# A two-layer trunk on one core: P·V read in 256 columns, kept weights and a new bank order in the output projection, two squares summed on TensorE, separate buffers for outgoing sums

## The chip, the core and the metric

The kernel runs on one core of a Trainium2 chip. The metric is the device time of one execution in microseconds (us). Beside the timed runs there is one profiled execution, whose trace gives every time that is read from a row below. The engines are called as in the profile: PE is TensorE (PEld its weight loads), DVE VectorE, ACT ScalarE, POOL GpSimd, SP SyncE. L12 is line 12 of the kernel.

## The reference

Sixteen learned tokens are put ahead of 1024 frames of width 1024; two layers follow. Each layer normalises, projects, runs two groups of heads side by side (a gated linear attention and FoX, a softmax attention with eight heads of 64 and a cumulative forget-gate bias), joins them in one output projection with a residual, and adds a gated feed-forward part with a causal convolution of width 3.

```python
for i in range(DEPTH):
    xn = rms_norm(h, attn_norm[i])
    gq, gk, gv, gr, glr, fq, fk, fv, ff = jnp.split(xn @ w_in[i], cuts, axis=-1)
    ...
    h = h + jnp.concatenate([o_gla, o_fox], axis=-1) @ w_out[i]
    h = h + conv_ffn(rms_norm(h, ffn_norm[i]), w_up[i], conv_w[i], conv_b[i], w_down[i])
return rms_norm(h, final_norm)[:, N_META:]
```

In conv_ffn a product with w_up gives u and g, each is convolved, and silu(g) * u is multiplied by w_down. In FoX the logits are q·k plus c_t − c_s, where c is the cumulative sum of the log forget gates, and the output is softmax(logits) · V.

## The kernel before

**Numbers.** Every fp32 operand is held as two parts, hi = cast(x) and lo = x − hi. A product is three matmuls into one bank of PSUM (mm3): hi·hi on L218, lo·hi on L219, hi·lo on L220. So a weight is loaded by SP into a buffer raw, cast to hi on ACT and subtracted to lo on DVE (weights: L185 and L187), one tile of 128 output columns ahead of its use (stream). In attention it is POOL that subtracts.

**Stages of a layer.** Projections and the linear attention; FoX attention; output projection with the second norm's statistics; up-projection; down-projection. In layer 0 attention lies at 176 to 539 us of the trace, the output projection at 539 to 601, up until 1048, down until 1258.6; in layer 1 attention at 1452 to 1815.5, the projection until 1879, up until 2328.6, down until 2537.

**FoX.** Queries and keys are cut into nine tiles, the first of 112 frames (FIRST) and the others of 116 (FT), and queries go in pairs of tiles, the first one alone. For each head and pair, fox_scores makes scores and probabilities P; fox_transposes turns P through PE, four key tiles at a time, into one tile of PSUM (tr, L690) and splits it into hi and lo in the buffer PT (L332 on ACT, L333 on DVE); fox_av multiplies (L708). PT has the layout key tile, hi or lo, query. A key tile that both query tiles see is read with 232 columns, one that only the second sees with 116. The steps of scores, transposes and P·V are put a few steps apart by fox_schedule, other work (the remaining projections, named mm) fills between them, and within that the framework's scheduler sets the order on each engine.

**Output projection** (the first half of ffn_up). The 1040 frames are two halves h of 520 (516 in layer 1, and 512 in its down-projection), each written in two chunks of half that. Eight tiles m of 128 output columns run per half, in the order (4, 0, 5, 1, 6, 2, 7, 3) in the first half and (0, 4, 1, 5, 2, 6, 3, 7) in the second. Tiles 4 to 7 need eight pieces of weights, in two loads, two casts and two subtractions, in each half anew; of tiles 0 to 3 all but the last piece was multiplied during attention. wout(i, h) takes bank i % 4, adds the residual (L1110), writes h out by POOL (L1111), squares it on ACT (L1116) and adds the squares on DVE (L1117). scale(h) sums over partitions by a matmul with ones (ssq, L1086, in bank 3), and DVE turns that into the norm's factor (L1089 and the rsqrt, L275 to L277). In the second half scale(0) runs after i = 1, and from i = 3 the first operands of up are normalised (first_operand, L1094, L1052, L1053). second_half calls scale(1) within up, then further operands follow (make_t2 and others).

**Down-projection** (down_blocks). Blocks of seven products, in the manner of Strassen's, run in the order of a table; copies on ACT and additions on DVE (L1375, L1376) gather them into two sums u and g per block, and a DMA on POOL adds those to h in memory (L1392, L1394). u and g come from the common slots, from which a generator (prepare) also takes its buffers: it loads gated activations (st, L1261) and splits them into ah and al (L332, L333) for the products to come. pump(n, keep) lets it go n steps if enough slots are free beside keep.

Of the kernel before, what the change touches and what calls it, by code (L numbers as in the profile page):

```python
# [10 lines left out]
F32 = mybir.dt.float32  # L11
# [40 lines left out]
NSPLIT = 4  # L52
# [82 lines left out]
class Kern:  # L135
# [33 lines left out]

    def weights(self, src, slots=None):  # L170
        nc = self.nc
        nk = src.shape[1]
        parts = []
        if slots:
            HI, LO = slots
        for k0 in range(0, nk, 4):
            n = min(4, nk - k0)
            raw = self.wp.tile([128, 4, 128], F32, tag="raw", name="raw", bufs=4)
            nc.sync.dma_start(raw[:, :n, :], src[:, k0:k0 + n, :])
            if slots:  # L180
# [4 lines left out]
            nc.scalar.copy(hi[:, :n, :], raw[:, :n, :])  # L185
            eng = nc.gpsimd if self.att else nc.vector
            eng.tensor_tensor(out=lo[:, :n, :], in0=raw[:, :n, :], in1=hi[:, :n, :].bitcast(F32), op=ALU.subtract)  # L187
            for k in range(n):
                parts.append((hi[:, k, :], lo[:, k, :]))
        return parts  # L190
# [485 lines left out]
    def fox_transposes(self, i, ci, P, PT, qoff, pp):  # L676
# [10 lines left out]
        for j in range(nt):  # L687
            t = 4 * ci + j
            o, w = self.start_of(t) - self.start_of(4 * ci), FT if i else FIRST
            nc.tensor.transpose(tr[:w, j, :rows], P[:rows, o:o + w], id_)  # L690
        self.split(PT[ci][:w, :nt, 0, qs], PT[ci][:w, :nt, 1, qs], tr[:w, :nt, :rows])

    def fox_av(self, e, tiles, q, PT, avs, pp, part):
# [5 lines left out]
        width = FT * (len(tiles) - 1) + self.rows_of(last)  # L699
        for t in range(4 * part, min(4 * part + 4, last + 1)):  # L700
            a = 0 if t <= tiles[0] else FT
            for i in range(2):
                if t == NT - 1:
                    w, x = q["Vm"][:, e, :, :], PT[2][:, i, :]
                else:
                    r = self.rows_of(t)
                    w, x = q["V"][e][:r, t, :, :], PT[part][:r, t - 4 * part, i, a:width]
                nc.tensor.matmul(av[:, a:width], w.rearrange("p a b -> p (a b)"), x,  # L708
                                 start=(t == 0 and i == 0), stop=(t == last and i == 1))
        if last < 4 * part + 4:  # L710
# [117 lines left out]
    def fox_schedule(self, lyr, at, n, p, e, ti, i, tiles, Ps, st, q, ap, pp, mix3):  # L828
        PT = st[e]

        def T_(ci, P):
            def f():
                if ti == len(tiles) - 1 and ci == 0:
                    for key in range(2):
                        PT[key] = ap.tile([FT, 4, 2, 2 * FT], F32R, tag=f"PT{key}", name=f"PT{key}", bufs=1)
# [196 lines left out]
    def ffn_up(self, lyr, mix, hT, pp, fw, halves, o0, during_last):  # L1032
# [49 lines left out]
        def scale(h):  # L1082

            ps, r = bank2("ssq", 3), acc[:, sl[h]]
            for c in range(2):
                nc.tensor.matmul(ps[:, c, :n], self.ones[:], acc[:, halves[h] + c * n:halves[h] + c * n + n],  # L1086
                                 start=True, stop=True)
            vv, y0, a = half(tmp[0], 0), half(tmp[0], 1), half(tmp[1], 0)
# [9 lines left out]
        def wout(i, h):  # L1098
# [3 lines left out]
            def f(w):  # L1102
                if h == 1 and i == KD - 1:
                    ensure(0)
                ps = bank2("wo", i % 4)
                for k in range(len(w)):
# [7 lines left out]
                else:  # L1114
                    t = half(sq, i % 2)
                    nc.scalar.activation(t, x, AF.Square)  # L1116
                    nc.vector.tensor_tensor(out=acc[:, sl[h]], in0=acc[:, sl[h]], in1=t, op=ALU.add)  # L1117
                if h == 0:
# [10 lines left out]
                for k in turn.get(i, ()):  # L1129
                    first_operand(k)  # L1130
            return (self.wm[lyr, M_WO + m][:, k0:KD, :], f)
        self.stream([wout(i, h) for h in range(2) for i in range(KD)])
        for x in mix:
# [219 lines left out]
    def down_blocks(self, lyr, g0, ng, X, pp, fw, halves, after):  # L1353
# [14 lines left out]
        def ensure(i):  # L1368
            while len(ops) < min(i + 1, len(seq)):
                j, p = seq[len(ops)]  # L1370
                ops.append(self.block_operand(wd(2 * j), wd(2 * j + 1), nk, j, p, fw, raws, len(ops) % 2))

        def evacuate(j, p):
            q = st[j]
            add = lambda out, ps: nc.vector.tensor_tensor(out=two(out), in0=ps[:, :, :n], in1=two(out), op=ALU.add)  # L1375
            copy = lambda out: nc.scalar.copy(two(out), q["a"][:, :, :n])  # L1376
            if p == 1:
                q["u"] = s.get(F32, "du")
                copy(q["u"][:, t0])
# [4 lines left out]
            elif p == 7:  # L1384
                q["g"] = s.get(F32, "dg")
                copy(q["g"][:, t1])
                add(q["g"][:, t1], q["x"])
            elif p == 4:
                copy(q["g"][:, t0])
                nc.gpsimd.dma_start(self.hm[2 * j + 1][:, o0:T], q["g"][:, o0:T], accum_op=ALU.add)  # L1390
                s.put(q["g"])
            elif p == 3:  # L1392
                add(q["u"][:, t1], q["x"])
                nc.gpsimd.dma_start(self.hm[2 * j][:, o0:T], q["u"][:, o0:T], accum_op=ALU.add)  # L1394
                s.put(q["u"])
                del st[j]
        def run():
            for i, (j, p) in enumerate(seq):
# [291 lines left out]
```

## Time and profile before

| | |
|---|---|
| runs | 2592.44, 2593.43, 2593.51 us; median 2593.43 |
| profiled execution | 2591.4 us, its span in the trace 2589.6 us |
| PE busy | 2495.7 us of the span (96%) |
| DVE busy | 1786.6 us (69%) |
| ACT busy | 1288.4 us (50%) |
| POOL busy | 432.6 us (17%) |

A row of the timeline has the start of an instruction in us from the span's start, its recorded length, its engine, line and operation with the names of output and input, and in brackets, where the engine was idle before, for how long and what ended that. A PE row is longer than the distance from one matmul to the next, since matmuls overlap: what a stream costs is read from start to start. A row of the grouped lines has the line, the operation, its shapes and count, then the busy time in us and the mean in ns, then the idle time ahead of it with who ended it.

### The profile page before, as it was taken

What the parts mean: (1) busy time and instruction counts of PE and PEld (TensorE: products, weight loads), DVE (VectorE), ACT (ScalarE), POOL (GpSimd) and SP (SyncE); (2) the same over time, 40 slices, a digit from 0 to 9 for tenths busy, and PEclk for the clock granted to TensorE, in tenths of its full rate; (3) what the DMA queues carried; (4) which work ended last, traced back from release to release, by engine and by line L of the source; (5) the groups of instructions that cost most, each with busy time, mean ns of one, the idle gap of its engine ahead of it and who ended that gap; (6) DMA issues with size and microseconds to landing.
All of it is one profiled execution on the core that took longest, in us unless ns stands there. A gap on an engine that the chain in (4) does not pass through costs nothing.

```text
span 2589.6 us, 48743 instructions
## 1 busy us (share of the span) xinstructions
PE 2495.7 (96%) x19278; PEld 2424.9 (94%) x19278; DVE 1786.6 (69%) x3494; ACT 1288.4 (50%) x2745; POOL 432.6 (17%) x598
## 2 busy tenths in 40 slices
PE   8999999898999999999999999999999999999997
PEld 7988999898999999999999899998899999999997
DVE  7656776759877777853665666776697777777535
ACT  7336666635544445641443565665464444455312
POOL 4033334310000000100301233332100000001002
PEclk9999999999999999999999999999999999999998
DMA  3132134342322223863312222143423222257721
GB/s 125 65 89 60 51 93 127 109 145 89 110 75 87 79 79 129 200 165 107 110 50 67 72 78 76 57 146 114 148 70 114 78 74 86 76 162 179 196 61 67
DMA packets 119670, 263.03 MB, mean 102 GB/s; under 512 B 15008, under 2 KB 32672, under 8 KB 119440
## 3 DMA queue, kind: packets, MB, share of 16 engines
q1 hardware_dynamic: 95136, 184.89, 22.8%
q0 software_dynamic: 22432, 72.71, 10.1%
q8 instruction: 151, 2.47, 0.4%
q10 hardware_dynamic: 1872, 2.31, 0.3%
q14 instruction: 79, 0.65, 0.1%
HBM read 179.26 MB, written 67.81 MB: 95 GB/s over the span
## 4 chain that ended last, share of the span: by engine, by line
PE 62%; issue 16%; DVE 13%; ACT 4%; DMA 3%; POOL 1%; SPq 0%; DVEq 0%; POOLq 0%; ACTq 0%
PE mm L218 7%; PE mm L220 6%; PE mm L219 6%; PE up L218 5%; PE up L219 5%; PE up L220 5%; PE down L218 5%; PE down L219 5%; PE down L220 5%; PE av L708 2%; DVE S L657 2%; PE tr L690 2%; ACT P L669 1%; PE wo L218 1%; PE wo L219 1%
## 5 line engine op out<-in xcount | busy, mean ns | idle before, releaser
L218 PE MATMUL up<-x,hi 128*128 128x260 f32 (+1 forms) x2464 | 697.3, 283 | 2.3 <-ACT x L1052 1.6
L220 PE MATMUL up<-x,hi 128*128 128x260 f32 (+1 forms) x2464 | 695.8, 282 | 2.2 <-DVE x L1053 2.2
L219 PE MATMUL up<-x,lo 128*128 128x260 f32 (+1 forms) x2464 | 696.1, 283 | 0.8 <-DVE lo L1029 0.8
L220 PEld LDWEIGHTS up<-x,hi 128*128 128x128 f32 x2464 | 465.5, 189 | 3.1 <-DVE x L1053 3.1
L218 PEld LDWEIGHTS up<-x,hi 128*128 128x128 f32 x2464 | 464.4, 188 | 3.4 <-ACT x L1052 2.2
L219 PEld LDWEIGHTS up<-x,lo 128*128 128x128 f32 x2464 | 464.8, 189 | 1.0 <-DVE lo L1029 1.0
L1029 DVE TENSOR_TENSOR lo<-raw,hi 128x512 fp32r<-128x512 f32 x364 | 249.0, 689 | 171.3 <-ACT hi L1028 171.3
L218 PE MATMUL mm<-xh,hi 128*128 128x348 f32 (+4 forms) x1056 | 364.6, 345 | 0.0
L220 PE MATMUL mm<-xl,hi 128*128 128x348 f32 (+4 forms) x1056 | 340.1, 322 | 0.0
L219 PE MATMUL mm<-xh,lo 128*128 128x348 f32 (+4 forms) x1056 | 339.2, 321 | 0.0
L1028 ACT CAST hi<-raw 128x512 fp32r<-128x512 f32 x364 | 224.5, 620 | 145.0 <-PE up L220 87.4
L185 ACT CAST hi<-raw 128x512 fp32r<-128x512 f32 (+2 forms) x192 | 112.4, 587 | 201.4 <-PE down L220 114.2
L218 PEld LDWEIGHTS mm<-xh,hi 128*128 128x128 f32 x1056 | 200.2, 190 | 5.9 <-issue 5.3
L219 PEld LDWEIGHTS mm<-xh,lo 128*128 128x128 f32 x1056 | 200.1, 190 | 0.4 <-issue 0.3
L220 PEld LDWEIGHTS mm<-xl,hi 128*128 128x128 f32 x1056 | 198.9, 188 | 0.3 <-issue 0.3
L219 PE MATMUL down<-ah,lo 128*128 128x260 f32 (+1 forms) x704 | 198.6, 282 | 0.3 <-DVE lo L187 0.3
L220 PE MATMUL down<-al,hi 128*128 128x260 f32 (+1 forms) x704 | 198.3, 282 | 0.0
L218 PE MATMUL down<-ah,hi 128*128 128x260 f32 (+1 forms) x704 | 198.3, 282 | 0.0
L669 ACT ACTIVATE P<-S,m 116x460 f32<-116x460 f32 (+2 forms) x224 | 124.8, 561 | 100.1 <-DVE m L657 97.9
L333 DVE TENSOR_TENSOR PT<-tr,PT 116x464 fp32r<-116x464 f32 (+3 forms) x240 | 123.0, 516 | 63.2 <-ACT PT L332 62.3
L1222 POOL DMA_DIRECT2D actd<-cv x44 | 23.6, 535 | 763.5 <-DVE cv L1221 742.5
L1011 DVE TENSOR_TENSOR raw<-raw,raw 128x512 f32<-128x512 f32 x198 | 129.9, 689 | 22.4 <-DMA raw<-in_wd_dram 18.4
(276 smaller groups left out, 5901.0 us busy)
## 6 DMA issues: line engine op xcount, KB each, us to landing
raw<-in_wm_dram SPq DMA_DIRECT2D x338, 256.0 KB, 2.8
raw<-in_wd_dram SPq DMA_DIRECT2D x64, 256.0 KB, 3.5
actd<-cv POOLq DMA_DIRECT2D x22, 520.0 KB, 3.0
actd<-cv POOLq DMA_DIRECT2D x22, 512.0 KB, 3.0
cb<-cd SPq DMA_DIRECT2D x16, 520.0 KB, 3.8
st<-actd SPq DMA_DIRECT2D x14, 520.0 KB, 4.8
st<-actd SPq DMA_DIRECT2D x14, 512.0 KB, 5.3
kA<-kA SPq DMA_DIRECT2D x24, 260.0 KB, 4.3
```

Source lines behind the costliest of these rows:

```text
L185: nc.scalar.copy(hi[:, :n, :], raw[:, :n, :])
L218: nc.tensor.matmul(ps, wh, xh[:, c0:c0 + n], start=first, stop=False, skip_group_check=more)
L219: nc.tensor.matmul(ps, wl, xh[:, c0:c0 + n], start=False, stop=False, skip_group_check=more)
L220: nc.tensor.matmul(ps, wh, xl[:, c0:c0 + n], start=False, stop=last, skip_group_check=more)
L333: nc.vector.tensor_tensor(out=lo, in0=src, in1=hi.bitcast(F32), op=ALU.subtract)
L657: nc.vector.tensor_tensor_reduce(out=S[:rows, :n], in0=S[:rows, :n], in1=cb[:rows, c0:k1], scale=1.0, scalar=(BIG if ci == 0 else m[:rows, ...
L669: nc.scalar.activation(P[:rows, :n], S[:rows, :n], AF.Exp, scale=-1.0, bias=m[:rows, nch - 1:nch], accum_out=(den if nch == 1 else d3[:row ...
L690: nc.tensor.transpose(tr[:w, j, :rows], P[:rows, o:o + w], id_)
L708: nc.tensor.matmul(av[:, a:width], w.rearrange("p a b -> p (a b)"), x, start=(t == 0 and i == 0), stop=(t == last and i == 1))
L1011: nc.vector.tensor_tensor(out=q[out][:, :nk, :], in0=q[a][:, :nk, :], in1=q[b][:, :nk, :], op=op)
L1028: nc.scalar.copy(hi[:, :nk, :], src[:, :nk, :])
L1029: nc.vector.tensor_tensor(out=lo[:, :nk, :], in0=src[:, :nk, :], in1=hi[:, :nk, :].bitcast(F32), op=ALU.subtract)
```

## The change

Four edits go together.

1. **P·V.** PT's layout becomes hi or lo, key tile, query, and the four key tiles lie in reverse order. Where both query tiles see a key tile and another tile's data lie behind it, the matmul reads 256 columns: its own 232 and 24 of the neighbour. The 24 extra columns of av aren't copied out. In the first part the order of key tiles is 1, 0, 2, 3, so that the matmul that starts the sum is one of 256 columns. 448 matmuls become longer; 192 keep 232 columns, since their tile lies last.
2. **Output projection.** Banks in the second half go (0, 1, 2, 0, 1, 3, 2, 1) instead of i % 4. The split weights of m = 5 and m = 6 are kept from the first half in buffers of the feed-forward pool (tags raw2, hi2, lo2) and used again in the second.
3. **Squares.** In the second half the squares of the last two tiles aren't added to the others on DVE; scale(1) sums the three parts in PSUM with three matmuls per chunk in place of one.
4. **Down.** u and g come from a ring of four buffers (do) that goes back to the slots only at the end of run, and both calls of pump lose their keep.

```diff
@@ weights
-    def weights(self, src, slots=None):
+    def weights(self, src, slots=None, keep=None):
...
+            elif keep:
+                hi, lo = (keep[0].tile([128, 4, 128], F32R, tag=t, name="keep", bufs=b) for t, b in keep[1])
@@ fox_transposes
-            nc.tensor.transpose(tr[:w, j, :rows], P[:rows, o:o + w], id_)
-        self.split(PT[ci][:w, :nt, 0, qs], PT[ci][:w, :nt, 1, qs], tr[:w, :nt, :rows])
+            nc.tensor.transpose(tr[:w, 3 - j, :rows], P[:rows, o:o + w], id_)
+        at = slice(4 - nt, 4)
+        self.split(PT[ci][:w, 0, at, qs], PT[ci][:w, 1, at, qs], tr[:w, at, :rows])
@@ fox_av
+        if part == 0 and last:
+            ts[:2] = 1, 0
...
+                    if a == 0 and p < 3:
+                        b = 256
+                        x = PT[part][:r, i].rearrange("p a b -> p (a b)")[:, 2 * FT * p:2 * FT * p + b]
+                nc.tensor.matmul(av[:, a:b], w.rearrange("p a b -> p (a b)"), x,
@@ scale
+            parts = [r] + [half(sq, i) for i in range(2) if h]
             for c in range(2):
-                nc.tensor.matmul(ps[:, c, :n], self.ones[:], acc[:, halves[h] + c * n:halves[h] + c * n + n],
-                                 start=True, stop=True)
+                for i, x in enumerate(parts):
+                    nc.tensor.matmul(ps[:, c, :n], self.ones[:], x[:, c * n:c * n + n],
+                                     start=i == 0, stop=i == len(parts) - 1)
@@ wout
-                ps = bank2("wo", i % 4)
+                ps = bank2("wo", (0, 1, 2, 0, 1, 3, 2, 1)[i] if h else i % 4)
...
+                    if not (h and i >= KD - 2):
+                        nc.vector.tensor_tensor(out=acc[:, sl[h]], in0=acc[:, sl[h]], in1=t, op=ALU.add)
...
+        keep = {5: (fw, [("raw2", 7)] * 2), 6: (fw, [("hi2", 3), ("lo2", 3)])}
@@ down_blocks
+        def outgoing():
+            if not ring:
+                ring.extend(s.get(F32, "do") for _ in range(4))
+            ring.append(ring.pop(0))
+            return ring[-1]
...
-                q["u"] = s.get(F32, "du")
+                q["u"] = outgoing()
...
-                    self.pump(1, 3)
+                    self.pump(1)
                 elif j and p == 5:
-                    self.pump(1, 4)
+                    self.pump(1)
+            s.put(*ring)
```

The lines of the kernel after are 3 to 38 higher than before. Three places show how the order moves. First DVE, near the end of the projection's second half: lo is the split of weights (L187 before, L190 after), h<-wo the residual's addition, h<-h,vec,r and x the operands of up, r<-r,sq the sum of squares, L1029 and L1040 the weights of up. Before:

```order
L1110 TENSOR_TENSOR h_5939<-wo,h_5939 128x520
L1053 TENSOR_TENSOR x_7525<-h_7065,x_7523 128x520
L1123 SCALAR_TENSOR_TENSOR dd<-h_5939,vec,gt 128x520
L1117 TENSOR_TENSOR r<-r,sq 128x520
L1053 TENSOR_TENSOR x_7520<-h_5933,x_7518 128x520
L187 TENSOR_TENSOR lo<-raw,hi 128x512 x2
L1110 TENSOR_TENSOR h_5936<-wo,h_5936 128x520
L1094 SCALAR_TENSOR_TENSOR h_5934<-h_5934,vec,r 128x520
L1029 TENSOR_TENSOR lo<-raw,hi 128x512
L1117 TENSOR_TENSOR r<-r,sq 128x520
```

And in the kernel after:

```order
L1123 TENSOR_TENSOR h_5939<-wo,h_5939 128x520
L1064 TENSOR_TENSOR x_7525<-h_5939,x_7523 128x520
L1138 SCALAR_TENSOR_TENSOR dd<-h_5939,vec,gt 128x520
L1132 TENSOR_TENSOR r<-r,sq 128x520
L1107 SCALAR_TENSOR_TENSOR h_7065<-h_7065,vec,r 128x520
L1107 SCALAR_TENSOR_TENSOR h_5933<-h_5933,vec,r 128x520
L190 TENSOR_TENSOR lo<-raw,hi 128x512
L1064 TENSOR_TENSOR x_7525<-h_7065,x_7523 128x520
L1064 TENSOR_TENSOR x_7520<-h_5933,x_7518 128x520
L1123 TENSOR_TENSOR h_5936<-wo,h_5936 128x520
L1107 SCALAR_TENSOR_TENSOR h_5934<-h_5934,vec,r 128x520
L1040 TENSOR_TENSOR lo<-raw,hi 128x512 x2
```

One lo of the last weights stands ahead of two operands where two stood behind them, and the second sum of squares is gone from this piece. The second place is ACT in the down-projection of layer 0, about the copy that frees a bank (du before, do after); ah is the cast of the activations. Before:

```order
L1028 CAST hi<-raw 128x512
L185 CAST hi<-raw 128x512
L332 CAST ah<-st 128x1040 x3
L1376 COPY du<-down 128x520
L332 CAST ah<-st 128x1040 x2
```

After:

```order
L1039 CAST hi<-raw 128x512
L335 CAST ah<-st 128x1040
L188 CAST hi<-raw 128x512
L335 CAST ah<-st 128x1040
L1415 COPY do<-down 128x520
L335 CAST ah<-st 128x1040 x2
```

Two casts of activations stand ahead of the copy in place of three, and a cast of weights lies between them. The third place is PE in attention, one pass of P·V (av) with the scores S of another step and the transposes tr. Before:

```order
L708 MATMUL av<-PT_2540,V_1609 128x232 x6
L654 MATMUL S<-kA_1605,qA_1603 116x460
L708 MATMUL av<-PT_2540,V_1609 128x232
L655 MATMUL S<-kL_1607,qA_1603 116x460
L708 MATMUL av<-PT_2540,V_1609 128x232
```

After:

```order
L719 MATMUL av<-PT_2540,V_1609 128x256 x2
L719 MATMUL av<-PT_2540,V_1609 128x232 x2
L719 MATMUL av<-PT_2540,V_1609 128x256 x2
L657 MATMUL S<-kA_1605,qA_1603 116x460
L719 MATMUL av<-PT_2540,V_1609 128x256
L658 MATMUL S<-kL_1607,qA_1603 116x460
L719 MATMUL av<-PT_2540,V_1609 128x256
```

Six of eight matmuls are longer; their place among the others is the same here.

More of the change, by code (lines that the diff above doesn't have):

```diff
@@ L699, in fox_av @@
         width = FT * (len(tiles) - 1) + self.rows_of(last)
-        for t in range(4 * part, min(4 * part + 4, last + 1)):
-            a = 0 if t <= tiles[0] else FT
+        ts = list(range(4 * part, min(4 * part + 4, last + 1)))
+        if part == 0 and last:
+            ts[:2] = 1, 0
+        for t in ts:
+            a, b = 0 if t <= tiles[0] else FT, width
             for i in range(2):
@@ L1130, in f, with wout_weights @@
                     first_operand(k)
-            return (self.wm[lyr, M_WO + m][:, k0:KD, :], f)
-        self.stream([wout(i, h) for h in range(2) for i in range(KD)])
+            return f
+        keep = {5: (fw, [("raw2", 7)] * 2), 6: (fw, [("hi2", 3), ("lo2", 3)])}
+        kept = {}
+        def wout_weights(h, i):
+            m = orders[h][i]
+            if m in kept:
+                return kept.pop(m)
+            w = self.weights(self.wm[lyr, M_WO + m][:, KD - 1 if m < NSPLIT else 0:KD, :], keep=keep.get(m))
+            if m in keep:
+                kept[m] = w
+            return w
+        todo = [(h, i) for h in range(2) for i in range(KD)]
+        ahead = wout_weights(*todo[0])
+        for this, nxt in zip(todo, todo[1:] + [None]):
+            w, ahead = ahead, nxt and wout_weights(*nxt)
+            wout(this[1], this[0])(w)
         for x in mix:
@@ L1384, in evacuate @@
             elif p == 7:
-                q["g"] = s.get(F32, "dg")
+                q["g"] = outgoing()
                 copy(q["g"][:, t1])
```

13 lines of the change are left out of this document (5 added, 8 removed).

## Prediction

> **What bounds the kernel now.** The sum is made against the profiled execution: 2591.4 us, of which the span in the trace is 2589.6; the median of the runs is 2593.43, 2.0 more, and is added at the end. First comes the page's table of busy time.
>
> ```profile
> PE 2495.7 (96%) x19278; PEld 2424.9 (94%) x19278; DVE 1786.6 (69%) x3494; ACT 1288.4 (50%) x2745; POOL 432.6 (17%) x598
> ```
>
> TensorE (PE) is at work nearly all the time, so every matmul that is added costs its length, and what can be won is the 4% in which PE stands still. The view of windows tells where that is. Its columns are the window, its length, the busy time of PE, PEld, DVE, ACT and POOL, the granted clock, the DMA share and GB/s. The rows are, in layer 0: attention; output projection; start of the up-projection; its rest; down-projection.
>
> ```profile
> 176.00:539.00 363.00, 340.93 (x2377) 324.53 (x2376) 246.64 (x762) 219.57 (x660) 126.11 (x177) 1.00 0.29 90
> 539.00:601.00 62.00, 56.45 (x438) 55.59 (x439) 44.97 (x75) 29.44 (x54) 9.05 (x16) 0.94 0.48 144
> 601.00:660.00 59.00, 56.08 (x455) 54.76 (x454) 58.28 (x88) 36.26 (x58) 2.88 (x4) 1.00 0.24 68
> 660.00:1048.00 388.00, 388.00 (x3248) 388.00 (x3248) 295.71 (x377) 194.06 (x278) 11.55 (x21) 1.00 0.30 99
> 1048.00:1258.60 210.60, 208.07 (x1732) 207.44 (x1731) 114.27 (x152) 75.39 (x117) 14.43 (x17) 1.00 0.55 144
> ```
>
> Attention lacks 22 us of PE, the projection 5.6 with a clock of 0.94, the start of up 2.9 while DVE is busy for 58.28 of 59 us, the rest of up nothing, down 2.5. So in the 120 us after attention DVE sets the pace, and everywhere else PE or the chain of softmax does. The timeline of PE shows the waits of the projection's second half (start, length, engine, line, operation, then in brackets the idle time and who ended it).
>
> ```profile
> 572.91 0.28 PE L220 MATMUL wo<-ml,hi 128*128 128x260 f32 x1
> 575.05 0.36 PE L218 MATMUL wo<-mh,hi 128*128 128x260 f32 x1 [1.86 <-DVE nt L1089]
> ...
> 576.33 0.42 PE L219 MATMUL wo<-mh,lo 128*128 128x260 f32 x1
> ...
> 579.59 0.35 PE L219 MATMUL wo<-mh,lo 128*128 128x260 f32 x1
> ...
> 590.32 0.28 PE L218 MATMUL wo<-mh,hi 128*128 128x260 f32 x1
> 593.82 0.59 PE L219 MATMUL wo<-mh,lo 128*128 128x260 f32 x1 [3.21 <-DVE lo L187]
> 594.20 0.42 PE L220 MATMUL wo<-ml,hi 128*128 128x260 f32 x1
> ...
> 596.80 0.28 PE L220 MATMUL wo<-ml,hi 128*128 128x260 f32 x1
> ...
> 604.46 1.11 PE L1086 MATMUL ssq<-r,ones 128*128 128x260 f32 x4 [0.59 <-DVE r L1117]
> ```
>
> Matmuls otherwise start every 0.12 us. After each of the two long waits they start every 0.22: the 15 starts up to 579.59 take 3.26 us where 1.80 would do, the 12 up to 596.80 take 2.60 instead of 1.44. A wait thus costs its own length and about 1.2 to 1.5 us more.
>
> **The output projection, step by step.** The new bank order takes the bank that DVE's L1089 reads out of the way of the fourth product: the wait of 2.0 us (575.05 − 572.91 − 0.12) and the slow 1.5 behind it go. The kept weights of m = 5 and 6 take away, in the second half of each layer, four loads, four ACT casts and four DVE subtractions (L187). Two of the eight sums of squares (L1117) leave DVE too. The timeline of DVE and the grouped lines of the 121 us give the prices.
>
> ```profile
> 580.26 0.69 DVE L187 TENSOR_TENSOR lo<-raw,hi 128x512 fp32r<-128x512 f32 x1 [1.32 <-ACT hi L185]
> ...
> 584.77 0.70 DVE L1117 TENSOR_TENSOR r<-r,sq 128x520 f32<-128x520 f32 x1
> 585.38 0.70 DVE L1053 TENSOR_TENSOR x<-h,x 128x520 fp32r<-128x520 f32 x1
> 585.99 0.69 DVE L187 TENSOR_TENSOR lo<-raw,hi 128x512 fp32r<-128x512 f32 x1
> 586.59 0.70 DVE L1110 TENSOR_TENSOR h<-wo,h 128x520 f32<-128x520 f32 x1
> ```
> ```profile
> L218 PE MATMUL up<-x,hi 128*128 128x260 f32 x150 | 42.8, 286 | 1.2 <-ACT x L1052 1.2
> L220 PE MATMUL up<-x,hi 128*128 128x260 f32 x150 | 42.5, 283 | 1.1 <-DVE x L1053 1.1
> L219 PE MATMUL wo<-mh,lo 128*128 128x260 f32 x144 | 42.4, 294 | 3.7 <-DVE lo L187 3.7
> ```
>
> DVE starts such an operation every 0.61 us though each is recorded with 0.70. Two accounts follow for one layer. On DVE: 4 × 0.60 for the subtractions, 2 × 0.61 for the sums, and the idle 1.32 at 580.26, which waits for the cast of a weight that is now kept: 4.9 us less from the second half's start to the last operand of up. On PE: 2.0 + 1.5 (first wait), 3.7 + 1.2 + 0.3 (the waits for lo, the slow stretch and the slow restart at 593.82), 0.6 before ssq, 2.3 in the start of up: 11.6 us that could go at most. Against it stand the squares that PE now adds itself: the four ssq matmuls hold PE from 571.43 to 572.12 and some.
>
> ```profile
> 571.43 1.04 PE L1086 MATMUL ssq<-r,ones 128*128 128x260 f32 x4
> 572.12 0.47 PE L218 MATMUL wo<-mh,hi 128*128 128x260 f32 x1
> 572.43 0.28 PE L219 MATMUL wo<-mh,lo 128*128 128x260 f32 x1
> ```
>
> Two fp32 matmuls are four records; by start to start of the last rows they take 0.69 to 0.87 us. Two squares more are eight records, +1.4 to +1.75 us of PE in each layer; I take 1.75. PE's account comes to −9.9 then, DVE's to −4.9. Up's first products wait for DVE, not the other way, and the last such wait is what shifts all the rest of the layer: the smaller of the two counts, **−4.9 a layer, −9.8 in all**. So PE's waits are not all gone: the second lo of m = 7's weights still stands behind a row of evacuations and operands on DVE. Ends: −8 a layer if up's operand sums, which the new order puts between the evacuations, fit in DVE's idle time; −1 if they push x back and only the two sums remain as gain. The loads and casts that go with the kept weights are counted at nothing more than this: both long waits end on DVE, and ACT is busy for 29.44 of the first 62 us.
>
> **P·V at 256 columns.** In each pass of a head, 28 of its 40 matmuls of 232 columns become 256; over 16 of these, 448 of the 640 in these two rows. All 640 and the price:
>
> ```profile
> L708 PE MATMUL av<-PT,V 116*128 116x232 f32 x512 | 88.8, 275 | 0.8 <-DVE PT L333 0.8
> L708 PE MATMUL av<-PT,V 112*128 112x232 f32 x128 | 29.8, 303 | 3.0 <-DVE PT L333 2.1 <-ACT PT L332 0.7
> ```
> ```profile
> 292.84 1.05 PE L708 MATMUL av<-PT,V 116*128 116x232 f32 x8
> 293.74 0.46 PE L690 MATMUL tr<-ident,P 116*116 116x116 f32 x3
> ```
> ```profile
> 2479.89 0.28 PE L218 MATMUL down<-ah,hi 128*128 128x256 f32 x1
> ...
> 2480.95 0.28 PE L218 MATMUL down<-ah,hi 128*128 128x256 f32 x1
> ```
>
> Eight of 232 columns take 0.90 us, 0.112 each; nine starts of 256 columns take 1.06, 0.118 each. So 448 × 0.006 = **+2.7 us**, on the path, as PE is the bound between its waits. Nothing in the trace says that 232 columns run at a worse rate than 256, so no gain stands against it. Ends: 0, where the added columns fall into time in which PE would have waited (22 us of attention), and +5. The Trainium skill (TensorE: Matmul & The Clock Gate, Back-to-back issue gap) speaks against this edit more strongly: it gives N/2.4 + 2.5 ns for a warm, isolated matmul of N columns, 10 ns more for 256 than for 232. By it the 448 would cost 4.5 us; the rows above show 6 ns, and the sum keeps those.
>
> In attention the order on DVE, ACT and POOL shifts as well, since a scheduler places it. No row prices that; I take 0, with ±4 us as the ends, about a tenth of what PE lacks in attention, if layer 1's is like layer 0's 22 us.
>
> **Down.** The sums that leave get buffers of their own, and the preparation of the gated activations runs one step at a time between products. The timelines of PE (layers 0 and 1) and of ACT:
>
> ```profile
> 1155.38 0.28 PE L220 MATMUL down<-x,hi 128*128 128x260 f32 x1
> 1156.83 0.39 PE L218 MATMUL down<-x,hi 128*128 128x260 f32 x1 [1.17 <-ACT du L1376]
> ...
> 2436.96 0.38 PE L218 MATMUL down<-x,hi 128*128 128x256 f32 x1 [1.42 <-ACT du L1376]
> ```
> ```profile
> 1155.22 1.06 ACT L332 CAST ah<-st 128x1040 fp32r<-128x1040 f32 x1 [0.37 <-DMA st<-actd]
> 1156.19 0.58 ACT L1376 COPY du<-down 128x520 f32<-128x520 f32 x1
> ```
>
> The copy that frees PE's bank stands behind a cast of 1.06 us that itself waited for a load. In the new order that cast comes after the copy. PE's start moves by 1156.83 − 1155.38 − 0.12 = 1.3 us in layer 0, and by 1.4 and the same 0.2 of restart in layer 1: **−2.9 us**. Ends: −4 (smaller waits for the same buffers go too) and 0 (the copy meets another cast).
>
> **Sum.** 2591.4 − 9.8 + 2.7 − 2.9 = 2581.4, and with 2.0 to the median of runs 2583.4: about **2583 us**, −0.4%. Differences under 0.2% (5.2 us) are about what a measurement of this kernel can't tell from none: below 2588.2 is faster, above 2598.6 slower.
>
> **The rivals.**
> - *The start of up keeps its end.* The kept weights free DVE in the second half, but in the order up's operands (L1029, L1011) have moved between the evacuations, and DVE at 58.28 of 59 us has no room for what is early: x arrives as late as now. The 4.9 shrinks to 1, the price of 2 sums: 2591.4 − 2 + 2.7 − 2.9 + 2.0 = 2591, no change. For it: the DVE window. Against: the same operations are only earlier, and four of them do not exist any more. Chance 0.15.
> - *Down meets its loads.* Between one block and the next ACT has waited much longer than 0.37 for what the preparation needs:
>
> ```profile
> 1132.46 1.06 ACT L332 CAST ah<-st 128x1040 fp32r<-128x1040 f32 x1 [4.85 <-DMA hm<-dg]
> ```
>
>   ACT works in order; if the copy of u now stood behind such a cast in each layer, 2 × 4.85 would come in place of −2.9: 2591.4 − 9.8 + 2.7 + 9.7 + 2.0 = 2596, no change. Against it: with buffers of their own the outgoing sums are no longer what that cast waits for. Chance 0.05.
> - *Attention gets slower.* Its chain of scores, softmax, transposes and P·V has PE waiting in these groups of the view of waits (layer 0: engine, line, for whom, total us, times, longest):
>
> ```profile
> PE tr L690 <- DVE PT L333: 10.4, 10, 2.2
> PE S L654 <- ACT P L669: 5.7, 5, 1.5
> ```
>
>   If the shifted order and the longer P·V doubled the first group, ten more waits of 1.04 us in each layer would cost 20.8: 2581.4 + 20.8 + 2.0 = 2604, slower. It decides from 15.2 us on, 7 to 8 such waits a layer. For it: DVE and ACT rows change places all through attention, and PE has no work of its own to bridge a wait there. Against: the splits, transposes and P·V keep their number and their groups. Chance 0.08.
>
> **How the numbers follow.** Forecast 0.72 (its own range 2574 to 2590: −8 a layer, −4 in down and P·V at 0 give 2573; −3 a layer and +3 in attention give 2590), of which a little, 0.02, lies within 0.2% of now; rivals 0.15, 0.05 and 0.08. The range 2574 to 2595 takes in the first rival and leaves out the last and half of the second, with some 0.05 below. Faster: 0.70 and 0.04 of the first rival's lower end, 0.74. Slower: 0.08. Same: 0.18.
>
> **What would show it.** In the projection PE no longer waits for DVE's nt after its third product, and no matmuls at 0.22 us follow; the last wait of up's start comes about 5 us sooner after attention; ssq has eight more records a layer and no wait before them. In attention a stretch between 0 and 3 us longer in each layer, with 448 rows of 256 columns. In down, PE's waits for the copy of u at 1.2 and 1.4 us gone, those of 0.7 for the copy of g as now. Wrong it is if the 121 us after attention shrink by under 2 us a layer, or if attention moves by more than 4 us a layer either way.

## The result and the profile after

The changed kernel takes 2579.8 us (median of four runs, 2576.27 to 2583.94) against 2593.47 before: the ratio is 0.9939, interval 0.9925 to 0.9953, so 12 to 19 us faster. The profiled execution has a span of 2577.6 us in place of 2589.6. The forecast was 2583 us, from 2574 to 2595. The total is near it, but two of its parts are far off.

The page's busy times first. PE is busy for 5.6 us longer, with the wider matmuls of P·V and the squares that it adds, in a span that is 12.0 us shorter.

```profile
PE 2501.3 (97%) x19294; PEld 2430.9 (94%) x19294; DVE 1776.4 (69%) x3482; ACT 1279.6 (50%) x2737; POOL 432.4 (17%) x598
```

Next the windows of the kernel after, cut at the first matmul of each stage: attention, projection, up's start and down of layer 0, then attention, projection and down of layer 1 (columns as above).

```profile
179.71:531.99 352.28, 338.41 (x2334) 321.79 (x2331) 244.11 (x758) 218.51 (x655) 124.03 (x176) 1.00 0.29 88
531.99:586.04 54.05, 53.08 (x437) 52.65 (x437) 36.72 (x62) 22.18 (x42) 10.02 (x17) 1.00 0.53 165
586.04:645.00 58.96, 56.51 (x449) 54.74 (x448) 58.83 (x91) 38.03 (x62) 2.34 (x3) 1.00 0.25 73
1034.84:1248.91 214.07, 209.15 (x1731) 208.66 (x1729) 114.17 (x152) 74.72 (x117) 14.34 (x17) 0.99 0.55 144
1450.06:1801.87 351.81, 336.86 (x2333) 320.20 (x2330) 243.58 (x758) 218.20 (x655) 124.22 (x176) 1.00 0.29 88
1801.87:1858.28 56.41, 54.32 (x436) 53.92 (x437) 37.41 (x63) 23.51 (x45) 10.00 (x17) 0.98 0.51 164
2308.98:2526.34 217.36, 208.04 (x1730) 207.22 (x1729) 113.43 (x150) 73.94 (x115) 14.42 (x17) 0.98 0.52 133
```

Cut the same way, the kernel before has these rows for its two attentions and the down of layer 1 (its projections, so cut, are 61.97 and 63.70 us, its first down 210.50):

```profile
180.98:538.88 357.90, 335.84 (x2333) 319.86 (x2331) 243.21 (x755) 217.04 (x651) 125.06 (x177) 1.00 0.29 90
1458.12:1815.46 357.34, 335.76 (x2334) 319.75 (x2331) 242.85 (x755) 217.00 (x651) 125.22 (x177) 1.00 0.30 90
2328.57:2537.26 208.69, 205.33 (x1730) 204.29 (x1729) 112.22 (x149) 73.84 (x114) 14.41 (x17) 1.00 0.53 138
```

Read the second column. Attention is 5.6 and 5.5 us shorter although PE is busy for longer in it: what PE lacks falls from 22 to 14 us in layer 0 and to 15 in layer 1. The projection is 7.9 and 7.3 shorter, with its clock at 1.00 and 0.98; the up stage behind it is 1.6 and 1.3 longer (447.2 to 448.8 and 449.4 to 450.7), which together makes −6.3 and −6.0 a layer. Down is 3.6 and 8.7 us *longer*. The three sums are −11.1, −12.3 and +12.3.

In the second half of the projection only one long wait of PE is left in each layer, 0.97 us in layer 0 and 2.09 in layer 1. The squares that PE adds follow up's products without a wait (timeline of PE, both waits, then the squares in layer 0):

```profile
581.92 0.28 PE L221 MATMUL wo<-mh,hi 128*128 128x260 f32 x1
583.17 0.39 PE L222 MATMUL wo<-mh,lo 128*128 128x260 f32 x1 [0.97 <-DVE lo L190]
...
1854.30 0.39 PE L222 MATMUL wo<-mh,lo 128*128 128x258 f32 x1 [2.09 <-DVE lo L190]
```
```profile
589.12 0.60 PE L1099 MATMUL ssq<-r,ones 128*128 128x260 f32 x2
...
591.56 0.47 PE L221 MATMUL up<-x,hi 128*128 128x260 f32 x1
```

From the first of twelve ssq records to up's next matmul it is 2.44 us; four took 0.69 to 0.87, so the new eight cost 1.6 to 1.75, as reckoned. The last wait for an operand in the start of up (the two rows below, of the kernel before and of the kernel after) ends 103.7 us after the projection's first matmul before (538.88) and 97.4 us after it now (531.99), 6.4 sooner; in layer 1 it is 5.5 sooner. DVE stays busy for 58.83 of the 58.96 us there.

```profile
642.61 0.39 PE L220 MATMUL up<-x,hi 128*128 128x260 f32 x1 [0.39 <-DVE x L1053]
```
```profile
629.36 0.39 PE L223 MATMUL up<-x,hi 128*128 128x260 f32 x1 [0.38 <-DVE x L1064]
```

In down the waits have changed places and grown (PE in layer 0 and twice in layer 1, then ACT about the first of them):

```profile
1149.61 0.59 PE L221 MATMUL down<-x,hi 128*128 128x260 f32 x1 [4.24 <-ACT do L1415]
...
2356.23 0.39 PE L221 MATMUL down<-x,hi 128*128 128x256 f32 x1 [3.07 <-ACT do L1415]
...
2428.26 0.39 PE L221 MATMUL down<-x,hi 128*128 128x256 f32 x1 [4.15 <-ACT do L1415]
```
```profile
1139.67 0.59 ACT L1415 COPY do<-down 128x520 f32<-128x520 f32 x1 [0.42 <-PE down L223]
1145.58 2.02 ACT L335 CAST ah<-st 128x1040 fp32r<-128x1040 f32 x2 [5.31 <-DMA st<-actd]
...
1148.02 1.05 ACT L335 CAST ah<-st 128x1040 fp32r<-128x1040 f32 x1
1148.98 0.58 ACT L1415 COPY do<-down 128x520 f32<-128x520 f32 x1
```

The copy at 1139.67 is early now, as forecast. But the two casts that were moved behind it stand ahead of the *next* copy, and they wait 5.31 us for their loads. That is the second rival, whose price per layer was a wait of 4.85. At the next copy's product PE had waited 0.68 us before; now it waits 4.24 and 4.15. The wait of 3.07 in layer 1 stands at a product that had none.

The waits are not the whole price. Behind each of these three the granted clock is halved for 3.4 us, from the end of the wait on in layer 0 and 0.9 to 1.3 us later in layer 1; matmuls start 0.21 us apart there in place of 0.12, as behind the long waits of the old projection. That costs some 1.5 us each time. Two windows of layer 1 show the clock:

```profile
2357.50:2360.90 3.40, 3.40 (x19) 3.40 (x18) 2.64 (x5) 1.50 (x3) 0.00 (x0) 0.50 0.04 16
2429.20:2432.60 3.40, 3.40 (x18) 3.40 (x17) 1.23 (x1) 1.05 (x1) 0.00 (x0) 0.50 1.00 401
```

In layer 1 PE's waits of over 0.25 us sum to 9.3 us after and 3.4 before. The difference and twice 1.5 for the clock make 9 us, against the 8.7 by which the stage grew.

### The profile page after: what moved, and what is told of

It reads as the page before. It is cut to its first block, busy times and chain, and to the rows that moved or that the text cites. A ratio compares the mean times of both kernels' runs of the same rounds, so it can differ in the third digit from the quotient of the medians.

```text
span 2577.6 us, 48764 instructions
## 1 busy us (share of the span) xinstructions
PE 2501.3 (97%) x19294; PEld 2430.9 (94%) x19294; DVE 1776.4 (69%) x3482; ACT 1279.6 (50%) x2737; POOL 432.4 (17%) x598
## 4 chain that ended last, share of the span: by engine, by line
PE 63%; issue 16%; DVE 13%; ACT 4%; DMA 3%; POOL 1%; SPq 0%; DVEq 0%; POOLq 0%; ACTq 0%
PE mm L221 7%; PE mm L222 7%; PE mm L223 7%; PE up L221 5%; PE up L222 5%; PE up L223 5%; PE down L221 5%; PE down L222 5%; PE down L223 5%; PE av L719 2%; PE tr L693 2%; DVE S L660 2%; ACT P L672 1%; DVE x L1064 1%; PE S L657 1%
## 5 line engine op out<-in xcount | busy, mean ns | idle before, releaser
L1040 DVE TENSOR_TENSOR lo<-raw,hi 128x512 fp32r<-128x512 f32 x364 | 248.1, 686 | 178.3 <-ACT hi L1039 175.5
L188 ACT CAST hi<-raw 128x512 fp32r<-128x512 f32 (+2 forms) x176 | 102.2, 582 | 190.2 <-PE down L223 108.1
L672 ACT ACTIVATE P<-S,m 116x460 f32<-116x460 f32 (+2 forms) x224 | 124.9, 561 | 79.4 <-DVE m L660 75.7
L336 DVE TENSOR_TENSOR PT<-tr,PT 116x464 fp32r<-116x464 f32 (+3 forms) x240 | 123.4, 515 | 48.4 <-ACT PT L335 46.5
L221 PE MATMUL down<-x,hi 128*128 128x260 f32 (+1 forms) x448 | 128.8, 288 | 12.8 <-ACT do L1415 12.8
```

The lines of the kernel that those rows point to most:

```text
L221: nc.tensor.matmul(ps, wh, xh[:, c0:c0 + n], start=first, stop=False, skip_group_check=more)
L336: nc.vector.tensor_tensor(out=lo, in0=src, in1=hi.bitcast(F32), op=ALU.subtract)
L672: nc.scalar.activation(P[:rows, :n], S[:rows, :n], AF.Exp, scale=-1.0, bias=m[:rows, nch - 1:nch], accum_out=(den if nch == 1 else d3[:row ...
L1040: nc.vector.tensor_tensor(out=lo[:, :nk, :], in0=src[:, :nk, :], in1=hi[:, :nk, :].bitcast(F32), op=ALU.subtract)
```

## The experiments

Stage lengths below are read like those above, from the first matmul of one stage to that of the next. "Projection and up" runs from the first wo matmul to the first of down: 509.2 and 513.1 us before. The expectation of the run bank has 609.2 and 613.1 for it, 100 us too much; the differences that it argues with are not touched by that. In the three other kernels that leave this part alone the stage takes 507.5 to 511.3 us in layer 0 and 512.9 to 513.4 in layer 1.

**pv: the P·V edit alone.** The diffs of fox_transposes, fox_av and PT's layout as in the change, nothing else.

> Only the P·V edit (layout, key order and 256 columns) on the kernel before. Theory 1: the 448 wider matmuls change what the scheduler believes of P·V, it orders DVE and PE otherwise in attention, and the waits of 1.4 to 1.5 us that came back every 84 us go: attention shorter by about 5.6 us a layer as in the changed kernel's trace (357.9 to 352.3 and 357.3 to 351.8), in all about 2593.5 - 11 = 2582 us. Theory 2, the prediction's: each wider matmul costs 6 ns and the order is neutral: 2593.5 + 2.7 = 2596 us. Theory 3: the shorter attention comes from the other edits (weights loaded ahead of the projection): no change or +2.7.

Measured: ratio 0.9929 (0.9907 to 0.9951), median 2578.5 against 2595.5. Theory 1 holds: the attention of both layers shrinks as in the full change. The windows of its attention, and its two groups in the view of waits (layer 0):

```profile
179.32:530.51 351.19, 338.62 (x2333) 321.62 (x2330) 242.34 (x755) 216.57 (x651) 124.72 (x177) 1.00 0.30 92
1452.44:1803.14 350.70, 336.78 (x2333) 320.17 (x2332) 241.84 (x755) 216.53 (x651) 125.15 (x177) 1.00 0.30 92
```
```profile
PE tr L690 <- DVE PT L333: 3.9, 5, 2.2
...
PE S L654 <- ACT P L669: 2.0, 3, 0.9
```

**pv232: the same without the width.** Layout and key order as changed, each matmul at its own columns:

```diff
-                    if a == 0 and p < 3:
-                        b = 256
-                        x = PT[part][:r, i].rearrange("p a b -> p (a b)")[:, 2 * FT * p:2 * FT * p + b]
```

> The P·V edit on the kernel before with the new layout and key order, but every matmul at its own 232 columns. On DVE the order in attention is then that of the kernel before, row for row. Theory 1 (the width changes the order, the order is the gain): attention as before, 357.9 and 357.3 us, time 2593.5 within 1 us. Theory 2 (the layout itself is the gain, since a split now writes hi and lo as two dense blocks): attention shorter by 5 us a layer, 2583 us.

Measured: ratio 1.0008 (0.9995 to 1.0021). Attention is back at the old length and a little over it, and the same two groups of waits are back too:

```profile
179.43:539.43 360.00, 337.38 (x2333) 321.89 (x2331) 243.40 (x755) 218.18 (x651) 125.28 (x177) 0.99 0.29 90
1457.73:1817.12 359.39, 337.81 (x2333) 322.04 (x2330) 243.15 (x755) 217.87 (x651) 125.29 (x177) 0.99 0.30 90
```
```profile
PE tr L690 <- DVE PT L333: 11.6, 10, 2.2
...
PE S L654 <- ACT P L669: 5.8, 5, 1.8
```

So it is the width alone, and it is not PE that gets faster by it. The next row of the trace after joins seven matmuls under the shape of the first; five have 256 columns, and two, those of the first key tile, have 232. They take 0.82 us from start to start (207.81 to 208.63). With 0.112 for each of the two, that leaves 0.119 for a wider one.

```profile
207.81 0.98 PE L719 MATMUL av<-PT,V 116*128 116x256 f32 x7
208.63 0.26 PE L693 MATMUL tr<-ident,P 116*116 116x116 f32 x1
```

What differs between pv and pv232 beside the length of these matmuls is the order on the engines: with 232 columns the order of DVE, ACT and POOL in attention is that of the kernel before row for row; with 256 some 54 of DVE's 754 rows and 37 of ACT's 650 in a layer stand elsewhere. The timeline of DVE shows one of the places, where PE waited about 1.4 us (until 240, 325 and 409 us). First before, then after: L657 (after L660) takes the maximum of new scores, L333 (L336) splits transposed probabilities into PT, and the short rows are the normalisation of a finished pair.

```profile
236.70 0.16 DVE L275 SCALAR_TENSOR_TENSOR fa<-fy 116x4 f32<-116x4 f32 x1 [0.51 <-ACT fy L274]
...
237.70 0.52 DVE L657 CUSTOM_DVE_ANT_0 S<-S,cb 116x344 f32<-116x344 f32 x1
...
239.41 0.64 DVE L333 TENSOR_TENSOR PT<-tr,PT 116x464 fp32r<-116x464 f32 x1 [1.14 <-ACT PT L332]
```
```profile
235.32 0.52 DVE L660 CUSTOM_DVE_ANT_0 S<-S,cb 116x344 f32<-116x344 f32 x1
235.76 0.14 DVE L660 DVE_READ_ACCUMULATOR2_ANT m<- 116x1 f32 x1
235.92 0.16 DVE L278 SCALAR_TENSOR_TENSOR fa<-fy 116x4 f32<-116x4 f32 x1
...
236.66 0.49 DVE L747 TENSOR_TENSOR fon<-ff,fy 116x128 f32<-116x128 f32 x2
237.07 1.02 DVE L336 TENSOR_TENSOR PT<-tr,PT 116x464 fp32r<-116x464 f32 x2
```

On ACT the exponential (L669, after L672) and the cast of the transposed probabilities (L332, after L335) have changed places at this point. Again before, then after:

```profile
238.31 0.55 ACT L669 ACTIVATE P<-S,m 116x344 f32<-116x344 f32 x1 [1.64 <-DVE m L657]
...
238.84 0.54 ACT L332 CAST PT<-tr 116x464 fp32r<-116x464 f32 x1
```
```profile
235.79 0.53 ACT L335 CAST PT<-tr 116x464 fp32r<-116x464 f32 x1
236.22 0.55 ACT L672 ACTIVATE P<-S,m 116x344 f32<-116x344 f32 x1
```

Before, the maximum waits behind a chain of small rows that itself waits for ACT; ACT's exponential waits for the maximum, the cast of PT on ACT stands behind the exponential, DVE's split waits 1.14 us for that cast, and PE's next transposes wait for the split. After, the maximum goes ahead of the small rows and the cast ahead of the exponential, and the split follows without a gap. Over all kernels of this study the seven with 256 columns have attention stages of 350.6 to 352.8 us, the seven with 232 (the kernel before among them) 357.3 to 361.0; the means are 351.4 and 358.8, 7.4 us a layer apart. That the scheduler's own estimate of a matmul of 232 columns is what turns the order is argued from this, not shown.

**wo: the projection's edits alone.** Bank order, kept weights and squares as in the change.

> Only the output projection's edits (bank order, kept weights, two squares on TensorE) on the kernel before; P·V and down as before. Theory 1: all that the projection and up's start win in the changed kernel comes from these, -6.3 and -6.0 us a layer from the start of the projection to the end of up, -12.3 in all: 2581 us. Theory 2, the prediction's account on DVE: -4.9 a layer, 2583.7 us. Theory 3: some of it hangs on attention ending otherwise: -4 a layer or less, 2585.5 us or more. Attention itself stays at 357.9 and 357.3 us within 1 in each theory.

Measured: ratio 0.9957 (0.9942 to 0.9972), 2584.4 against 2595.5. Projection and up take 503.0 and 506.8, −6.2 and −6.3 a layer: theory 1. Attention is 360.6 and 361.0, outside the expected 1 us, but within what the old order shows in other kernels.

**kept, bank, sq: the three edits one by one.** Kept: only keep and kept of wout_weights. Bank:

```diff
-                ps = bank2("wo", i % 4)
+                ps = bank2("wo", (0, 1, 2, 0, 1, 3, 2, 1)[i] if h else i % 4)
```

Sq: only scale and the condition ahead of L1117.

> Only the kept weights of m = 5 and 6 on the kernel before. Theory 1, the prediction's account on DVE: four subtractions of 0.60 and the wait of 1.32 for a cast are gone, -3.7 a layer from the start of the projection to the end of up. Theory 2 (PE's waits add up for themselves): the waits for lo and the slow stretch behind them go, -5 a layer. In both, attention becomes longer by about 3 us a layer, as in the run of all projection edits (357.9 to 360.6 and 357.3 to 361.0), if the three kept subtractions that now stand on DVE near its end are what lengthens it; as before within 1.5 us if they are not. Together about 2593 or 2590 us with the longer attention, 2586 or 2583 without.

> Only the bank order of the projection's second half on the kernel before. Theory 1 (DVE sets when up's start is over, so what PE wins is waited for later): the wait of 1.9 us for L1089 goes, but projection and up together keep their 609.2 and 613.1 us within 1 us. Theory 2 (PE's waits add up for themselves): -2.0 and the slow 1.5 behind it, -3.5 a layer.

> Only the two squares on TensorE on the kernel before. Theory 1 (DVE sets the end): two sums fewer on DVE, -1.2 a layer in projection and up together, the 1.75 us of PE hidden in its waits. Theory 2 (PE pays): +1.75 for the eight ssq records, -0.6 for the wait ahead of them: +1.2 a layer.

Measured: kept 0.9975 (0.9963 to 0.9987), projection and up −3.1 and −4.6, near the −3.7 of DVE's account, and attention unchanged (358.0 and 358.1), so the kept subtractions do not lengthen it. Bank, one run: 507.9 and 510.4, −1.3 and −2.7, between its two theories; the −1.3 lies within the spread of this stage in layer 0, the −2.7 outside that of layer 1. Sq, one run: +4.8 and +1.0. The second number is theory 2's, PE paying for the records; the first isn't a price of the edit, since the window of up's start in layer 0 shows a granted clock of 0.94 for 59 us, where it was 1.00 before:

```profile
603.12:662.00 58.88, 56.66 (x434) 55.48 (x433) 53.36 (x83) 35.38 (x56) 2.32 (x3) 0.94 0.24 68
```

In layer 1 the three edits add up: −4.6 − 2.7 + 1.0 = −6.3, which is what all three give together. In layer 0 they would make +0.4 against −6.2, with the lost clock of sq among them, so that layer decides nothing. That the squares cost nothing once the other two edits are there is thus not shown; layer 1 speaks for their paying their price.

**down: the down edit alone.** The ring and both pump calls as in the change.

> Only the down edit (ring of four buffers, pump without keep) on the kernel before. Theory 1: the ring itself brings the loss that the changed kernel shows (down 210.5 to 214.1 and 208.7 to 217.4): the preparation runs further ahead, its loads stand on SP behind loads of h that wait for outgoing sums, and ACT's casts of activations, ahead of the copy that PE needs, wait for them: +12 us, 2605.5 us. Theory 2, the prediction's: the cast moves behind the copy, -2.9: 2590.5 us. Theory 3: the loss comes from the other edits, which bring down's start to another moment relative to its loads: between -3 and +2 us.

Measured: ratio 1.0046 (1.0029 to 1.0064), 2605.5 us. That is the time of theory 1, though against the 2595.5 us of the kernel before in the same comparison it is +10 by the medians and +12 by the ratio; the prediction's −2.9 is refuted. Down takes 213.2 and 215.9 us, 2.7 and 7.2 longer. PE waits 2.34 us at the product that has the 4.24 of layer 0, and 2.62 and 4.55 at those of layer 1.

**no_down: the change without its down edit.** down_blocks as before.

> The changed kernel without its down edit: u and g from the common slots, pump with keep. Theory 1 (the down edit costs 12 us): down back at 210.5 and 208.7 us, all else as in the changed kernel: 2593.5 - 13.7 - 12.2 = 2567.6 us, ratio 0.990. Theory 2 (the changed kernel's waits in down come from the rest of the change): down stays at 214 and 217 us, time about 2580 us.

Measured: ratio 0.9903 (0.9889 to 0.9916), median 2570.5: faster than both kernels by theory 1, some 9 us below the changed one. Down in layer 1 is back at 208.5. In layer 0 it is 212.7, but that stage varies from 210.5 to 214.1 in kernels that leave it alone, so only layer 1 (207.4 to 208.8 in those) decides anything. Its waits in layer 1 (ACT's for a load, then PE's), to be read against 2428.26 above:

```profile
2415.69 1.05 ACT L335 CAST ah<-st 128x1024 fp32r<-128x1024 f32 x1 [0.36 <-DMA st<-actd]
```
```profile
2415.38 0.38 PE L221 MATMUL down<-x,hi 128*128 128x256 f32 x1 [1.62 <-ACT du L1406]
2419.15 0.38 PE L221 MATMUL down<-x,hi 128*128 128x256 f32 x1 [0.67 <-ACT dg L1406]
```

**slots_pump, ring_keep: ring and pump apart.** In slots_pump the ring is gone and pump is free, in ring_keep the ring stays and pump has its keep:

```diff
-                    self.pump(1)
+                    self.pump(1, 3)
                 elif j and p == 5:
-                    self.pump(1)
+                    self.pump(1, 4)
```

> The changed kernel without the ring, u and g from the common slots as before, but pump without keep. Theory 1 (the freed pump is the loss): PE waits of 3 us and more in down as in the changed kernel, one run about 2578 to 2583 us. Theory 2 (the ring is the loss): down as before within 1 us a layer, one run about 2566 to 2570 us.

> The changed kernel with pump's keep of 3 and 4 put back; the ring stays. Theory 1 (it is the freed pump that puts casts ahead of the copies before their loads have come): the waits of 4.4, 3.2 and 4.3 us fall under 1.5 us, down 210 to 211 and 208 to 210 us, about 2569 us. Theory 2 (the ring alone does it, since it takes four slots from the preparation): the waits stay, about 2580 us or more.

Measured: slots_pump 2566.8 in its one run, down 212.0 and 208.5. Without the ring a free pump even leaves the order of PE, DVE, ACT and POOL as it is in no_down: keep held nothing back there. Ring_keep 0.9906 (0.9892 to 0.9919), which is not to be told from no_down; down 210.0 and 211.9. In layer 1 two of the three waits stay above the 1.5 us that theory 1 asked for, and down is 3.4 us longer than in no_down:

```profile
2350.58 0.38 PE L221 MATMUL down<-x,hi 128*128 128x256 f32 x1 [2.65 <-ACT do L1415]
...
2419.40 0.38 PE L221 MATMUL down<-x,hi 128*128 128x256 f32 x1 [2.30 <-ACT do L1415]
```

So neither part alone costs a time that can be measured here. The loss of the changed kernel needs the ring and the free pump together; the ring with keep still brings a part of it to layer 1, which layer 0, with 210.0 at the lower end of its spread, makes up for.

**pool_res and ring_back: why the loads are late.** In the changed kernel SP waits, in the window from 1120 to 1152 us, above all in two places: for an outgoing sum, on a load of h (L1473) that stands ahead of the activations' loads, and for a product of PE, on a load of activations (L1291):

```profile
SPq L1473 <- DMA hm<-do: 9.9, 1, 9.9
SPq L1291 <- PE down L223: 9.4, 2, 8.2
```

pool_res takes these loads of h off SP:

```diff
-                nc.sync.dma_start(hT[k][:, o0:T], self.hm[k][:, o0:T])
+                nc.gpsimd.dma_start(hT[k][:, o0:T], self.hm[k][:, o0:T])
```

> The changed kernel with one edit: the loads of h for the residual in down are issued by POOL instead of SP. ACT's order in down stays that of the changed kernel. Theory 1 (the activations' loads come late because they stand on SP behind loads of h that wait for the outgoing sums): PE's waits of 4.4 us at 1145 and 4.3 us at 2424 go or fall under 1.5 us, about 2580 - 7 = 2573 us; the wait of 3.2 us at 2353 in layer 1, which has no load of h ahead of it, stays. Theory 2 (the loads are late for lack of a free buffer or of DMA, whatever stands ahead on SP): the waits stay above 3.5 us, about 2580 us.

ring_back gives two of the ring's buffers to the slots early:

```diff
                 q = st.setdefault(j, {})
+                if (j, p) == (NP - 1, 2):
+                    s.put(ring.pop(1), ring.pop(1))
```

> The changed kernel, but two of the ring's four buffers go back to the slots when the last block's first product starts, instead of all four at the end. Theory 1 (the ring holds slots, so that the loads of the next activations wait on SP for slots that PE frees later, and ACT's casts for the loads): PE's waits of 4.4 us at 1145 and 4.3 at 2424 fall to about 1.5 and 1.8, as without the ring; the wait of 3.2 us at 2353, ahead of the last block, stays: about 2580 - 5.4 = 2574 us. Theory 2 (order alone: casts stand ahead of the copy, whenever the slots come free): waits stay above 3.5 us, 2580 us.

Measured: pool_res 0.9925 (0.9907 to 0.9943), its waits of PE 2.49 and 3.85 in place of 4.24 and 4.15; SP's wait for DMA is gone, and those of L1291 for PE are 14.0 us in place of 9.4:

```profile
1149.61 0.39 PE L221 MATMUL down<-x,hi 128*128 128x260 f32 x1 [2.49 <-ACT do L1415]
...
2423.05 0.58 PE L221 MATMUL down<-x,hi 128*128 128x256 f32 x1 [3.85 <-ACT do L1415]
```
```profile
SPq L1291 <- PE down L223: 14.0, 4, 8.2
```

ring_back 0.9934 (0.9918 to 0.9950), no better than the change itself; in both layers the wait is cut in two, 0.89 and 2.04 us in layer 0, 0.92 and 3.02 in layer 1.

Neither expectation's first theory comes out. In layer 1 taking the loads of h off SP leaves the wait nearly as it was; that they are a part of it in layer 0 isn't shown either, since the run down, which leaves them on SP, waits 2.34 us at the same product. With the loads of h gone from the queue, the activations' loads wait for PE instead. Giving two buffers back doesn't do it alone. What is shown is the chain at its end (late load, cast on ACT, copy behind it, PE) and that the ring together with the free pump starts it. Which of their effects on the order makes the load late stays open.

## Why the prediction came out right, step by step

The total was right by luck: two large steps were wrong in opposite directions, by some 14 and 15 us. By one of the prediction's own signs it was wrong: attention was not to move by more than 4 us a layer, and it moved by 5.6 and 5.5. Its other sign, that the projection and the start of up shrink by at least 2 us a layer, held.

- **Projection, DVE's account of −4.9 a layer:** right in where the time is won, a little small: −6.2 to −6.3 alone, −6.3 and −6.0 within the change, and the last wait for an operand of up comes 6.4 and 5.5 us sooner. Of its terms that for the kept weights (3.7) is confirmed by itself, −3.1 and −4.6. The two others missed in opposite directions in layer 1: the edit of the squares, counted at −1.2 for two sums less on DVE, came out as +1.0, and the bank order, counted at nothing beyond that account, gave −2.7. That a product which PE starts sooner is also evacuated sooner, so that the account on DVE isn't closed against PE, would explain the bank order; it is argued, not shown.
- **One wait left for m = 7's lo:** right, 0.97 us in layer 0 and 2.09 in layer 1. The squares at 1.75 us of PE, covered by freed waits: right in price, but that they are covered isn't shown; in layer 1 the three edits add up with the squares at +1.0.
- **P·V, +2.7 us:** the price of a wider matmul is nearly right, 0.119 against 0.112 (the term took 0.118, from rows of the down-projection). By the formula that the Trainium skill (TensorE: Matmul & The Clock Gate, Back-to-back issue gap) gives for an isolated matmul it would be dearer by 10 ns, an estimate; the trace shows 7.
- **"In attention the order ... No row prices that; I take 0, with ±4 us":** this step failed. Attention became 11 us shorter within the change and 13 in pv, although its matmuls are wider, and the bound was 4. The rows to see it by were there: waits of PE for L333 that summed to 10.4 us in ten places, with DVE's maximum behind small rows in the timeline. The order of the changed kernel has that maximum ahead of them. Bounding by a tenth of the lack was a guess with no wait behind it; the group of waits, 10 to 16 us a layer, was the bound to take, downward too.
- **Down, "in the new order that cast comes after the copy", −2.9:** failed. The reading of the first copy was right, and the casts behind it were not followed to the next copy, nor their loads on SP to what frees their slots. The edit alone is +12 us by its ratio. The rival with this mechanism had a chance of 0.05 and the right size for its wait (4.85; measured 4.24 and 4.15), and the argument against it, that the outgoing sums no longer hold what the cast waits for, did not save it: the casts waited for loads all the same.
- **Attention slower:** the third rival had the right place and the wrong sign. PE's waits for L333 fell from ten to six in layer 0, 10.4 to 4.8 us, instead of doubling.

## What to carry to other kernels

Where a scheduler places the instructions, an edit's price includes what it does to the order, and that can be several times its own length. Look for it as a list of waits in the trace of before and ask of each whether the new order puts its releaser earlier; take the sum of these waits as the bound on both sides.

A row that is moved behind one consumer stands ahead of the next. Follow it there, and follow its inputs back through the queue that loads them, before counting a stall as gone.

Where a change has several edits, time each alone, and also the whole without each: here the change without its down edit is better than the whole, at a ratio of 0.990, and two parts of that edit, which apart cost no time that could be measured (one of them in a single run), cost 9 us together.

## What was not expected of the hardware

Two sizes. Waits of 2 to 4 us were mostly followed by a lower clock, and so cost more than their length. With most of them gone the projection has a clock of 1.00 and 0.98 in the two layers, where it was 0.94 and 0.92; what is left in layer 1 follows its wait of 2.09 us, and down, which has got such waits, falls to 0.99 and 0.98. Not every such wait is followed by it: in ring_keep, with waits of 2.65 and 2.30 us, down keeps 1.00. The kernel sq also lost clock in the 59 us of up's start (0.94), about 3 us; why is not shown. And timed runs of the kernel before span 2590.4 to 2601.1 us over the study, wider than the three runs shown ahead of the change (2592.4 to 2593.5) suggest, so that 0.2% needs more runs than three.
